# Three SwiGLU half-steps of a two-layer backbone: five groups of four tiles by quarters, and two plain tiles at the end

## The chip, the cores and the metric

The kernel runs on one core of one Trainium2 chip. The metric is the device time of one launch in microseconds (us). Engines are named as in the profile: PE is the matrix engine, PEld its weight loads, DVE the vector engine, ACT the scalar engine, POOL the third elementwise engine, SP the queue that issues most of the transfers.

## The reference, cut to what matters

Two layers run over 512 latent tokens and 256 context tokens. Each layer is a half-step SwiGLU, a token mixing, and a second half-step SwiGLU; every one of them begins with an RMSNorm that is scaled and shifted, and ends with a gated addition.

```python
def _swiglu(h, w_gu, w_down):
    a, b = jnp.split(h @ w_gu, 2, axis=-1)
    return (jax.nn.silu(a) * b) @ w_down
...
h_lat = h_lat + 0.5 * ml[2] * _swiglu(_modulate(h_lat, norm_ffn1[l], ml[0], ml[1]), ffn1_w_gu[l], ffn1_w_down[l])
h_ctx = h_ctx + 0.5 * mc[2] * _swiglu(_modulate(h_ctx, norm_ffn1[l], mc[0], mc[1]), ffn1_w_gu[l], ffn1_w_down[l])
...
mix_lat, mix_ctx = _token_mix(n_lat, n_ctx, w_in[l], w_out[l], ...)
h_lat = h_lat + ml[5] * mix_lat
h_lat = h_lat + 0.5 * ml[8] * _swiglu(_modulate(h_lat, norm_ffn2[l], ml[6], ml[7]), ffn2_w_gu[l], ffn2_w_down[l])
```

The width is 1024, the hidden width of SwiGLU 2816, which is 22 tiles of 128. The context takes no part in the second SwiGLU of layer 1, so three half-steps have 768 tokens and one has 512.

## The kernel before, in words

**Numbers.** Every float32 operand is split into a rounded high part and the remainder, and a product takes three matmuls (`mm3`: high by high, high by low, low by high). A weight tile of 128x512 arrives by a transfer into a `raw` buffer (four of them), ACT casts its high part into a `w` buffer (eight of them), and DVE or POOL subtracts to get the low part (`w_copies`, `w_subs`).

**By quarters.** A product of two operands that are cut in halves both ways needs eight block products; the kernel uses a scheme with seven and some sums before and after. The gate and up products of a pair of hidden tiles are done so (`pair`: the inner dimension and the tokens are halved, 384 tokens each; sums of the activations are made once per half-step by `t_task`, sums of the weights by POOL in `w_sums`). The first pair of a half-step is done plainly (`first_pair`), because those sums are not there yet. The down product of four hidden tiles is also done by quarters where `fast` says so: `hid_sums` forms the seven combinations of the hidden tiles (`put` splits each into high and low), `down_fast` multiplies each with its weight combination and DVE adds it to the residual `H` (`upd`). Such a group of four has 7 x 2 x 2 outputs of 128 features by 384 tokens with 2 x 3 matmuls each, which is 168 matmuls of 384 columns. The sums of its weights are POOL's.

**Plain.** Otherwise `down` multiplies the hidden tiles of the group for one output of 128 features after the other. A group in the middle does it in two chunks of 384 tokens; the last group does it in three chunks of 256 (HALF0 and HALF1 of the latent tokens, then the context, CTX), and as soon as the eight outputs of a chunk are added to `H`, the next step's norm of that chunk starts: `norm_sq` squares on ACT and sums into `nacc`, `norm_r` transposes `nacc` on PE, reduces on DVE and takes the root on POOL (`rs`), `norm_task` transposes `rs` on PE and then, for each of eight feature tiles, scales (DVE), adds the shift (DVE or ACT), casts the high part (ACT) and subtracts (DVE or POOL). PE's first products of the next step read these tiles.

**What sets the order.** The order of every engine's instructions is fixed when the kernel is written out: generators yield when the program's own estimate of time says that something is not ready, and what comes first in that estimate is written first. Each engine then runs its list in order and waits on semaphores. `segs` names the groups of a half-step: first all pairs of a segment, then its down products. Before, layer 0 uses `[(2, 4), (4,), (4,), (4,), (4,)]` and layer 1 `[(2,), (4,), (4,), (4,), (4,), (4,)]`; the rule is

```python
return n == 4 and f + n < NF and (l, which) != (1, 2)
```

so in each of the three half-steps with 768 tokens the first two tiles go down plainly, 16 by quarters, and the last four plainly in three chunks. `u` is the ring of 20 large buffers that holds activations, their sums and hidden tiles.

Of the kernel before, what the change touches and what calls it, by code (L numbers as in the profile page):

```python
# [10 lines left out]
F32R = mybir.dt.float32r  # L11
# [4 lines left out]
P = 128  # L16
# [7 lines left out]
PROJ = 2304  # L24
EPS = 1e-6
NMOD = 9
SEGA, SEGB = [(2, 4), (4,), (4,), (4,), (4,)], [(2,), (4,), (4,), (4,), (4,), (4,)]

LAT = (0, 512, 0)
CTXC = (512, 256, 1)  # L30
# [110 lines left out]
class Kernel:  # L141
# [8 lines left out]
    def __init__(self, tc, I, out, pools):  # L150
# [10 lines left out]
        self.flags = set()  # L161
        self.mcols = [16, 0]
        self.mod0 = self.rawlim = 0
        self.ulive = 0
        self.nready = {}
        self.ps = pools["ps"].tile([P, 4096], F32, tag="b", name="b", bufs=1)
# [428 lines left out]
        return n == 4 and f + n < NF and (l, which) != (1, 2)  # L595

    def segs(self, l, which):
        return SEGA if l == 0 else SEGB


    def setup(self):
# [554 lines left out]
    def hid_tiles(self, quick, f, hid):  # L1156

        if not quick or f == 0:
            x = yield from (self.uget([P, 4, self.tq]) if quick else self.uget([P, 2, TOK], F32R))
            hid.append(x)  # L1160
        return hid[-1]

# [57 lines left out]
    def pair(self, l, which, i, hid, done, quick):  # L1220
# [4 lines left out]
        def prod(no, nm, h, out, start):  # L1225
            yield (lambda: nm in self.R)
            w = yield from self.getp(("u", l, which, i, no, h))
            hi, lo = self.R[nm]
            for j in range(4):
                r = self.rdy(lo[:, j])  # L1230
                if r > self.t:
                    yield r
                c = slice(j * P, j * P + P)
                self.mm3(out[:, :tq], (w[:, 0, c], w[:, 1, c]), (hi[:, j], lo[:, j]), start and j == 0, j == 3, True)
                yield
            self.relp(w)

        def work(f, th):

# [131 lines left out]
    def ffn(self, l, which, chunks, last_chunks, next_norm):  # L1371
# [5 lines left out]
        for si, ns in enumerate(segs):  # L1377
            last = si == len(segs) - 1
            groups, i = [], f
            for n in ns:  # L1380
                hid, done, sums, quick = [], [], {}, self.fast(l, which, n, i)
                if quick:
                    self.spawn(self.hid_sums(hid, done, tq, sums), 1)
                for i in range(i, i + n, 2):
                    self.spare = i + 4 - f <= 4
                    yield from (self.pair(l, which, i, hid, done, quick) if i else self.first_pair(l, which, hid, done, quick))
                i += 2
                groups.append((n, quick, hid, done, sums))
# [6 lines left out]
            for n, quick, hid, done, sums in groups:  # L1395
# [14 lines left out]
                                if cc == order[-1] and (kt + 1) * P % w == 0:  # L1410
                                    self.relp(Ws[kt * P // w])
                else:
                    for hi, lo in self.R.values():
                        self.uf(hi, lo)
                    if which == 1:
                        self.spawn(self.mix_constants(l), 3)
                    Ws = []
# [860 lines left out]
```

## Time and profile before

| | |
|---|---|
| median of three runs | 2637.1 us (2631.66 to 2638.93) |
| the profiled execution's own time | 2629.54 us |
| its span | 2627.8 us |
| PE busy | 2539.9 us (97%) |
| DVE / POOL / ACT busy | 2033.7 (77%) / 1322.7 (50%) / 1249.9 us (48%) |
| mean granted clock of PE | 0.99 |

The page gives busy time per engine, then the span in forty slices (the granted clock in tenths of full speed), the queues of transfers, the chain of waits that ended last, and groups of instructions with their count, busy time, mean duration and the idle time before them. The three half-steps lie at 45 to 594 us, 923 to 1480 us and 1480 to 1982 us; the mixings lie between them and after the third.

### The profile page before, as it was taken

The numbers are of one execution on the slowest core, as the hardware profiler recorded it, in microseconds if no ns is written. First come the engines' busy times: TensorE is split into PE (matmuls) and PEld (weight loads), VectorE is DVE, ScalarE is ACT, GpSimd is POOL, SyncE is SP. The second block draws the span as 40 slices with busy tenths as digits, with TensorE's granted clock in tenths as the row PEclk, the third lists the DMA queues.
The fourth block names the chain that finished last, engine by engine and source line by source line (L and its number), as shares of the span: only waits on it lengthen the run. The fifth ranks groups of instructions, "written<-read, shape, count | busy, mean of one in ns | idle before, by whom it ended". The sixth has DMA issues, their size and how long they took to land.

```text
span 2627.8 us, 44905 instructions
## 1 busy us (share of the span) xinstructions
PE 2539.9 (97%) x17116; PEld 2418.3 (92%) x17116; DVE 2033.7 (77%) x3513; ACT 1249.9 (48%) x2576; POOL 1322.7 (50%) x1093
## 2 busy tenths in 40 slices
PE   7999999999999999999999989999999999999998
PEld 5888999999998978889999989999999888999998
DVE  5767787878689886776787877878878788977776
ACT  4433344456645643343444534444446655544445
POOL 3636656733232344555774547767744332644443
PEclk9999999999999999999999999999999999999999
DMA  8455322221121155553223112222222211233332
GB/s 283 141 184 180 113 73 89 65 83 57 49 65 33 57 170 176 185 170 133 76 65 97 49 49 81 65 65 75 74 87 65 61 57 40 66 96 98 99 103 72
DMA packets 193623, 252.58 MB, mean 96 GB/s; under 512 B 12188, under 2 KB 160896, under 8 KB 193408
## 3 DMA queue, kind: packets, MB, share of 16 engines
q1 hardware_dynamic: 187152, 246.82, 29.3%
q10 hardware_dynamic: 6256, 2.90, 0.4%
q8 instruction: 134, 2.20, 0.3%
q14 instruction: 81, 0.66, 0.1%
HBM read 247.59 MB, written 2.10 MB: 95 GB/s over the span
## 4 chain that ended last, share of the span: by engine, by line
PE 69%; DVE 19%; issue 3%; POOL 3%; ACT 3%; DMA 2%; SPq 0%; ACTq 0%; DVEq 0%; POOLq 0%
PE b L241 42%; PE b L243 23%; DVE u L127 8%; DVE w L127 4%; DVE t L127 4%; PE b L254 2%; DVE H L127 2%; PE b L282 2%; DMA raw<-in_ffn_w_gu_dram 1%; ACT u L127 1%; POOL w L127 1%; POOL raw L127 1%; ACT w L127 1%; ACT t L127 1%; POOL nacc L127 0%
## 5 line engine op out<-in xcount | busy, mean ns | idle before, releaser
L241 PE MATMUL b<-u,w 128*128 128x384 f32 (+1 forms) x8736 | 1447.1, 326 | 13.9 <-DVE adasum L127 6.8
L241 PEld LDWEIGHTS b<-u,w 128*128 128x128 f32 x8736 | 1425.6, 189 | 33.7 <-issue 16.7
L127 ACT CAST w<-raw 128x512 fp32r<-128x512 f32 x949 | 575.6, 620 | 572.0 <-PE b L241 199.9
L127 DVE TENSOR_TENSOR w<-raw,w 128x512 fp32r<-128x512 f32 x677 | 651.2, 972 | 233.7 <-ACT w L127 226.5
L127 POOL TENSOR_TENSOR raw<-raw 128x512 f32<-128x512 f32 x416 | 612.8, 1494 | 344.6 <-DMA raw<-in_ffn_w_gu_dram 125.7
L127 POOL TENSOR_TENSOR w<-raw,w 128x512 fp32r<-128x512 f32 x272 | 374.1, 1390 | 501.3 <-ACT w L127 454.7
L243 PE MATMUL b<-u,w 128*128 128x256 f32 (+2 forms) x3888 | 584.4, 308 | 21.8 <-ACT u L127 6.4
L243 PEld LDWEIGHTS b<-u,w 128*128 128x128 f32 x3888 | 542.6, 193 | 46.7 <-ACT u L127 7.7
L127 DVE SCALAR_TENSOR_TENSOR H<-b,modG,H 128x128 f32<-128x128 f32 (+3 forms) x832 | 364.3, 473 | 135.1 <-PE b L243 80.5
L243 PE MATMUL b<-w,u 128*128 128x256 f32 x2172 | 281.2, 286 | 1.3 <-DVE w L127 1.2
L243 PEld LDWEIGHTS b<-w,u 128*128 128x128 f32 x2172 | 271.2, 193 | 6.5 <-DVE w L127 1.7
L127 ACT CAST u<-u 128x384 fp32r<-128x384 f32 (+4 forms) x318 | 140.7, 464 | 133.0 <-DVE u L127 86.6
L127 DVE TENSOR_TENSOR u<-u 128x384 fp32r<-128x384 f32 (+8 forms) x226 | 167.9, 763 | 11.6 <-ACT u L127 10.7
L127 POOL TENSOR_TENSOR u<-u 128x384 fp32r<-128x384 f32 (+3 forms) x138 | 120.1, 880 | 95.3 <-ACT u L127 94.9
L127 ACT CAST u<-t 128x384 fp32r<-128x384 f32 (+2 forms) x162 | 74.8, 471 | 187.8 <-DVE t L127 183.1
L127 ACT COPY t<-b 128x384 f32<-128x384 f32 (+5 forms) x223 | 99.3, 446 | 122.3 <-PE b L241 78.7
L127 POOL TENSOR_TENSOR nacc<-nacc,t 128x256 f32<-128x256 f32 (+2 forms) x112 | 90.5, 808 | 102.5 <-ACT t L127 98.4
L127 DVE TENSOR_TENSOR t<-t,b 128x384 f32<-128x384 f32 (+3 forms) x216 | 105.9, 493 | 33.8 <-PE b L241 33.2
L127 DVE TENSOR_TENSOR u<-u,t 128x384 f32<-128x384 f32 (+1 forms) x105 | 102.0, 979 | 12.9 <-POOL u L127 4.8
L127 DVE TENSOR_TENSOR u<-t,u 128x384 fp32r<-128x384 f32 (+3 forms) x144 | 101.3, 709 | 10.6 <-ACT u L127 9.3
L243 PE MATMUL b<-u 128*128 128x256 f32 (+5 forms) x516 | 103.7, 334 | 3.4 <-DVE u L127 3.1
L127 DVE TENSOR_TENSOR u<-b,u 64x256 fp32r<-64x256 f32 (+3 forms) x175 | 90.9, 525 | 19.6 <-ACT u L127 17.8
(99 smaller groups left out, 1563.0 us busy)
## 6 DMA issues: line engine op xcount, KB each, us to landing
raw<-in_ffn_w_gu_dram SPq DMA_DIRECT2D x176, 512.0 KB
adaraw<-in_ada_w_dram SPq DMA_DIRECT2D x114, 512.0 KB
raw<-in_ffn_w_down_dram SPq DMA_DIRECT2D x88, 512.0 KB
raw<-in_w_in_dram SPq DMA_DIRECT2D x28, 512.0 KB
raw<-in_w_out_dram SPq DMA_DIRECT2D x32, 256.0 KB
u<-in_ada_w_dram SPq DMA_DIRECT2D x14, 512.0 KB
u<-in_ada_w_dram SPq DMA_DIRECT2D x16, 384.0 KB
raw<-in_w_in_dram SPq DMA_DIRECT2D x16, 256.0 KB
```

What stands on the lines that cost most here:

```text
L127: getattr(self.eng, name)(*args, **kw)
L241: self.nc.tensor.matmul(out, a, b, start=start, stop=stop, skip_group_check=True)
L243: self.nc.tensor.matmul(out, a, b, start=start, stop=stop)
L254: self.nc.tensor.matmul(out[q:q + 32], self.cs[:, k], x, start=start, stop=stop)
L282: self.nc.tensor.transpose(out, in_, self.ident[:p, :p])
```

## The change

The segments of the three half-steps become five groups of four, all by quarters, and the last segment has a plain group of two tiles behind its group of four: the pairs of all six tiles first, then the group's down product by quarters, then the two tiles plainly in the three chunks of 256 tokens. The first pair's hidden tiles now go down by quarters too. Two `u` buffers are taken at the start of the last segment for the plain tiles' hidden values, and the sums of the activations are given back one by one in the last pair instead of all at once behind it. The second SwiGLU of layer 1 keeps its segments.

```diff
-SEGA, SEGB = [(2, 4), (4,), (4,), (4,), (4,)], [(2,), (4,), (4,), (4,), (4,), (4,)]
+SEGF, SEGP = [(4,), (4,), (4,), (4,), (4, 2)], [(2,), (4,), (4,), (4,), (4,), (4,)]
...
     def segs(self, l, which):
-        return SEGA if l == 0 else SEGB
+        return SEGP if (l, which) == (1, 2) else SEGF
...
         if not quick or f == 0:
-            x = yield from (self.uget([P, 4, self.tq]) if quick else self.uget([P, 2, TOK], F32R))
+            if self.kept:
+                x = self.kept.pop(0)
+            else:
+                x = yield from (self.uget([P, 4, self.tq]) if quick else self.uget([P, 2, TOK], F32R))
             hid.append(x)
...
             self.relp(w)
+            if h == 1 and i == NF - 2:
+
+                self.uf(*self.R.pop(nm))
...
             groups, i = [], f
+            keep = []
+            if len(ns) > 1:
+
+                keep = yield from self.ugets(2, [P, 2, TOK], F32R)
...
                 for i in range(i, i + n, 2):
+                    self.kept = [] if quick else keep
...
                 else:
-                    for hi, lo in self.R.values():
-                        self.uf(hi, lo)
                     if which == 1:
```

**PE, end of layer 0's first half-step.** `u,w` with 256 columns are the plain down products, `nacc` and `rs` the two transposes of a chunk's norm, `w,u` the first projection of the mixing. Before:

```order
L241 MATMUL b<-u,w 128x384 x1488
L243 MATMUL b<-u,w 128x256 x111
L282 MATMUL b<-ident,nacc 128x128 x2
L243 MATMUL b<-u,w 128x256 x15
L282 MATMUL b<-ident,rs 128x128 x2
L243 MATMUL b<-u,w 128x256 x99
L282 MATMUL b<-ident,nacc 128x128 x2
L243 MATMUL b<-u,w 128x256 x18
L282 MATMUL b<-ident,rs 128x128 x2
L243 MATMUL b<-u,w 128x256 x45
L243 MATMUL b<-w,u 128x256 x42
L282 MATMUL b<-ident,nacc 128x128 x2
```

There are 288 plain matmuls. In the changed kernel there are 144 (75 and the first `nacc` stand ahead of these rows), and the context's two transposes stand between the first matmuls of the projection:

```order
L245 MATMUL b<-u,w 128x256 x18
L284 MATMUL b<-ident,rs 128x128 x2
L245 MATMUL b<-u,w 128x256 x48
L284 MATMUL b<-ident,nacc 128x128 x2
L245 MATMUL b<-u,w 128x256 x3
L245 MATMUL b<-w,u 128x256 x6
L284 MATMUL b<-ident,rs 128x128 x2
L245 MATMUL b<-w,u 128x256 x9
L284 MATMUL b<-ident,nacc 128x128 x2
L245 MATMUL b<-w,u 128x256 x9
L284 MATMUL b<-ident,rs 128x128 x2
L245 MATMUL b<-w,u 128x256 x120
```

The transposes of the first rotated projection (`ident,t`) follow directly behind the 120.

**DVE, the same place.** `u<-H,modA,b` is the scaling of a norm, `u<-u,M` its shift, `u<-u` its subtraction, `w<-raw,w` the low part of a weight tile. Before, the end of HALF1's updates:

```order
L127 SCALAR_TENSOR_TENSOR H<-b,modG,H 128x256 x2
L127 TENSOR_TENSOR w<-raw,w 128x512
L127 TENSOR_TENSOR nacc<-nacc,t 128x256
L127 SCALAR_TENSOR_TENSOR H<-b,modG,H 128x256
L127 TENSOR_TENSOR w<-raw,w 128x512
L127 TENSOR_REDUCE ms<-b 128x2
```

In the changed kernel, from the last update of the context on:

```order
L128 SCALAR_TENSOR_TENSOR H<-b,modG,H 128x256
L128 TENSOR_SCALAR modG<-M 128x16
L128 TENSOR_TENSOR w<-raw,w 128x512
L128 SCALAR_TENSOR_TENSOR u<-H,modA,b 128x256
L128 TENSOR_SCALAR u<-u,M 128x256
L128 TENSOR_TENSOR u<-u 128x256
```

At that point four of HALF0's eight scalings are still to come. From HALF0's last update to the end of the first rotation DVE's list has eight `w<-raw,w` before and four now.

**PE, from layer 0's second half-step into layer 1's first.** Before:

```order
L243 MATMUL b<-u,w 128x256 x45
L243 MATMUL b<-u,w 128x384 x42
L282 MATMUL b<-ident,nacc 128x128 x2
L243 MATMUL b<-u,w 128x384 x12
L282 MATMUL b<-ident,rs 128x128 x2
L243 MATMUL b<-u,w 128x384 x234
L241 MATMUL b<-u,w 128x384 x2352
```

Now:

```order
L245 MATMUL b<-u,w 128x256 x48
L284 MATMUL b<-ident,nacc 128x128 x2
L245 MATMUL b<-u,w 128x256 x3
L284 MATMUL b<-ident,rs 128x128 x2
L284 MATMUL b<-ident,nacc 128x128 x2
L284 MATMUL b<-ident,rs 128x128 x2
L245 MATMUL b<-u,w 128x384 x192
L243 MATMUL b<-u,w 128x384 x2520
```

The 96 plain down matmuls behind the first pair (42 + 12 + 234 are 192 of the pair and these 96) are gone, the 168 of the new group are among the 2520, and the context's transposes stand ahead of the first pair. Over the program PE has 432 matmuls of 256 columns fewer and 216 of 384 columns more; DVE has 30 `w<-raw,w` fewer, POOL 48 more of them and 24 more sums of raw tiles.

## Rows read from the trace of the kernel before

**Rows 1.** The page: busy time, share of the span, instructions of each engine.

```profile
PE 2539.9 (97%) x17116; PEld 2418.3 (92%) x17116; DVE 2033.7 (77%) x3513; ACT 1249.9 (48%) x2576; POOL 1322.7 (50%) x1093
```

**Rows 2.** The page's groups: line, engine, operation, count | busy us, mean ns | idle before.

```profile
L127 DVE TENSOR_TENSOR w<-raw,w 128x512 fp32r<-128x512 f32 x677 | 651.2, 972 | 233.7 <-ACT w L127 226.5
L127 POOL TENSOR_TENSOR raw<-raw 128x512 f32<-128x512 f32 x416 | 612.8, 1494 | 344.6 <-DMA raw<-in_ffn_w_gu_dram 125.7
L127 POOL TENSOR_TENSOR w<-raw,w 128x512 fp32r<-128x512 f32 x272 | 374.1, 1390 | 501.3 <-ACT w L127 454.7
```

**Rows 3.** PE's timeline: start us, length us, instructions merged [idle before <-releaser].

```profile
442.04 33.21 PE L241 MATMUL b<-u,w 128*128 128x384 f32 x190 [0.16 <-DVE u L127]
...
556.55 13.46 PE L243 MATMUL b<-u,w 128*128 128x256 f32 x111
569.86 0.42 PE L282 MATMUL b<-ident,nacc 128*128 128x128 f32 x2
...
595.07 3.02 PE L243 MATMUL b<-w,u 128*128 128x256 f32 x23 [0.62 <-DVE w L127]
598.45 0.44 PE L282 MATMUL b<-ident,nacc 128*128 128x128 f32 x2 [0.36 <-POOL nacc L127]
...
604.11 0.38 PE L282 MATMUL b<-ident,t 128*128 128x128 f32 x2
...
628.96 0.33 PE L282 MATMUL b<-ident,t 128*128 128x128 f32 x1 [1.81 <-DVE t L127]
```

**Rows 4.** DVE's timeline where layer 0's first half-step ends.

```profile
568.26 0.48 DVE L127 SCALAR_TENSOR_TENSOR H<-b,modG,H 128x256 f32<-128x256 f32 x1 [0.96 <-PE b L243]
...
572.33 1.26 DVE L127 SCALAR_TENSOR_TENSOR u<-H,modA,b 128x256 f32<-128x256 f32 x3 [0.45 <-PE b L282]
573.51 0.34 DVE L127 TENSOR_SCALAR u<-u,M 128x256 f32<-128x256 f32 x1
...
574.66 0.42 DVE L127 TENSOR_TENSOR u<-u 128x256 fp32r<-128x256 f32 x1
...
584.21 0.67 DVE L127 TENSOR_TENSOR w<-raw,w 128x512 fp32r<-128x512 f32 x1
...
611.38 0.42 DVE L127 TENSOR_TENSOR u<-u 128x256 fp32r<-128x256 f32 x1 [0.47 <-ACT u L127]
```

**Rows 5.** Stretches: length, busy of PE, PEld, DVE, ACT, POOL, granted clock, transfers.

```profile
168.00:221.00 53.00, 52.06 (x345) 47.33 (x346) 41.92 (x88) 15.93 (x30) 33.30 (x27) 1.00 0.48 166
386.10:474.30 88.20, 88.04 (x508) 87.72 (x507) 72.60 (x107) 38.69 (x76) 61.56 (x45) 1.00 0.24 72
568.70:611.80 43.10, 42.12 (x350) 41.61 (x349) 40.35 (x97) 26.69 (x65) 23.98 (x31) 1.00 0.17 50
1034.00:1077.00 43.00, 40.40 (x278) 35.59 (x277) 35.63 (x71) 12.27 (x23) 22.43 (x18) 1.00 0.37 124
1450.00:1481.80 31.80, 30.95 (x238) 30.40 (x237) 28.63 (x78) 20.93 (x58) 20.30 (x30) 1.00 0.01 2
1519.00:1537.00 18.00, 15.16 (x76) 14.76 (x77) 16.24 (x34) 3.00 (x5) 6.42 (x5) 0.81 0.01 2
1982.00:2022.00 40.00, 37.08 (x293) 36.20 (x291) 34.22 (x77) 25.84 (x56) 19.54 (x25) 0.96 0.23 67
```

**Rows 6.** PE's timeline, from the context's last norm to layer 1's first down product.

```profile
1482.22 0.44 PE L282 MATMUL b<-ident,nacc 128*128 128x128 f32 x2 [1.17 <-DVE nacc L127]
...
1483.13 2.20 PE L243 MATMUL b<-u,w 128*128 128x384 f32 x11 [0.29 <-POOL u L127]
...
1516.43 0.62 PE L243 MATMUL b<-u,w 128*128 128x384 f32 x2 [2.56 <-DVE u L127]
1520.12 0.69 PE L243 MATMUL b<-u,w 128*128 128x384 f32 x1 [3.07 <-ACT u L127]
1522.53 13.57 PE L243 MATMUL b<-u,w 128*128 128x384 f32 x68 [1.72 <-DVE u L127]
```

**Rows 7.** PE's timeline, first matmuls of the second pair in layer 0's two half-steps.

```profile
91.00 0.79 PE L241 MATMUL b<-u,w 128*128 128x384 f32 x3 [3.59 <-DVE adasum L127]
...
966.46 0.76 PE L241 MATMUL b<-u,w 128*128 128x384 f32 x3 [1.00 <-DVE adasum L127]
```

More of the change, by code (lines that the diff above doesn't have):

```diff
@@ L163, in __init__ @@
         self.mod0 = self.rawlim = 0
+        self.kept = []
         self.ulive = 0
```

## The prediction

> **What bounds the kernel now.** I read the page's busy times first: PE is busy 97% of the span and DVE 77% [rows 1], so time is won either by taking work from PE or by closing the places where PE waits. Then PE's timeline, to see how long a matmul takes and where the idle time stands; then the stretches, to see who is full where PE waits. In the middle of a half-step PE never stops: from 386 to 474 us, one group of four tiles with its two pairs, it is busy 88.04 of 88.20 us, while DVE is at 72.60 and POOL at 61.56 [rows 5]. At the ends it is otherwise. From the last update of HALF0 at 568.3 us to the end of the context's norm at 611.8 us [rows 4] DVE is busy 40.35 of 43.10 us and PE 42.12 [rows 5]: both are full there, and PE's own waits are small, 0.62 and 0.36 us [rows 3]. The same holds from 1450 to 1481.8 us, with 28.63 us of DVE in 31.80 [rows 5]. What I take from this: in the body of a half-step a matmul less is time won, and in the hand-over from one step to the next PE and DVE are two queues of almost equal length, so that shortening PE's alone wins only what DVE lets it win.
>
> **The change part by part.** The durations are those of the profiled execution, which took 2629.5 us and lies 7.6 us under the median of 2637.1. The sum below is a difference; I add it to the median.
>
> *Matmuls.* 190 matmuls of 384 columns take 33.21 us, 0.175 us each; 111 of 256 columns take from 556.55 to 569.86, 13.31 us, 0.120 us each [rows 3]. A half-step loses 96 of 384 columns (16.8 us) and 144 of 256 (17.3 us) and gets a group of 168 of 384 (29.4 us). That is 4.7 us less for each of three half-steps, **14.1 us less** in all, and all of it is on PE, which the chain follows.
>
> *DVE, ACT and POOL for the new group.* One more group by quarters means combinations of the hidden tiles, 28 wider updates in place of narrower ones, 24 more sums of raw weights over the program at 1494 ns and 48 more subtractions on POOL at 1390 ns [rows 2], 103 us of POOL in three half-steps, while DVE gives up 30 subtractions of 972 ns [rows 2]. I cost it at nothing: the same mix of work stands beside the group from 386 to 474 us, where DVE has 15.6 us and POOL 26.6 us to spare and PE none [rows 5]. If that cover were gone, 34 us of POOL per half-step would be the price. Transfers stay the same in bytes; buffers of `u` are given back earlier.
>
> *The first down product.* In layer 1 the two plain tiles go down behind a single pair, and PE stands still for their hidden tiles three times, 2.56, 3.07 and 1.72 us [rows 6]; the releasers are DVE and ACT, whose list is full of sums of activations at that time. Now a second pair follows, which does not need the hidden tiles: **7.4 us less**. In layer 0 the plain products behind three pairs show smaller waits: PE idles 0.94 us from 168 to 221 us and 2.60 us from 1034 to 1077 us [rows 5]. With them **3.5 us** go. In their place layer 1 gets the wait that both half-steps of layer 0 show at their second pair, 3.59 and 1.00 us [rows 7]; I take the mean, **2.3 us more**, and the two as its ends.
>
> *The hand-overs.* The plain tail shrinks from 288 to 144 matmuls, from about 35 to 17 us, but the work that DVE does in it stays: 24 updates, three norms, and the weights of what follows. The price is the difference of two queues. From HALF0's last update to the end of the norms and the first rotation DVE needs 40.35 us now [rows 5]. Four of its eight weight subtractions leave that stretch (4 x 0.97 = 3.9 us [rows 2]), and about 1.5 of its 2.75 us of idle time are the norm's chain, which stays: 38.0 us. PE has in the same stretch of the changed order 96 down matmuls and 144 of the projection, 28.8 us, and five pairs of transposes of 0.38 us [rows 3], 30.7 us in all. It waits 7.3 us where it waited 1.0 [rows 3]: **6.3 us more**. The hand-over of layer 1's first half-step is the same work, with granted clock and idle time as before (37.08 of 40 us busy) [rows 5]: **6.3 us more**. Between the layers DVE needs 28.63 us until HALF1's tiles stand [rows 5], less three subtractions (2.9 us) and plus 1.5 us, 27.2 us; PE has 96 x 0.120 + 48 x 0.175 us and four pairs of transposes, 21.4 us. It waits 5.8 us where it waited 1.17 and 0.29 [rows 6]: **4.3 us more**. Behind each, who waits is clear: PE's list has the first projection, or the first pair, right behind the transposes, and all else is queued behind those. The bounds: nothing, if DVE never holds PE longer than now (PE is busy 42.12 of 43.10 us there [rows 5]); and, if no subtraction leaves and all idle time stays, 43.1 - 30.7 - 1.0 = 11.4 us at the mixings and 31.8 - 21.4 - 1.5 = 8.9 us between the layers. I take the values above, since the rows of DVE's stretch are nearest to what is left in its list.
>
> *The granted clock.* In the two stretches with waits of PE it is 0.81 over 18 us and 0.96 over 40 us [rows 5]: part of the time the lower of the two levels, 1.2 GHz, was granted, which costs 3.4 and 1.6 us. Where PE has no waits it is 1.00. I let the new wait at the first mixing cost one such fall, **1.6 us more**, and leave the other two as they are; the ends are 3.4 us less and 6.8 us more.
>
> *The sum:* -14.1 - 7.4 - 3.5 + 2.3 + 6.3 + 6.3 + 4.3 + 1.6 = **-4.2 us**, 2632.9 us on the median: **2633 us**. A measurement of this kernel can tell about 0.3%, 7.9 us, from no change; so this is no change. With all lower ends it is -14.1 - 7.4 - 3.5 + 1.0 - 3.4 = -27.4 us, with all upper ends, the first downs' 3.5 us not won, -14.1 - 7.4 + 3.6 + 11.4 + 11.4 + 8.9 + 6.8 = +20.6 us.
>
> One row needs a word: a subtraction of DVE takes 0.67 us at 584.21 us [rows 4] and 0.97 us on average [rows 2], so something stretches it by 0.30 us. The Trainium skill, in SBUF — State Buffer, section "Who interferes with whom", says that a DVE instruction with two inputs in SBUF and a POOL instruction that reads SBUF exclude each other for their whole length, which speaks against moving work to POOL. By that rule each of the four subtractions that leave DVE at a hand-over would come back as one stretched instruction there; the trace has the stretch but not its cause.
>
> **The rivals.**
>
> *DVE yields (0.28).* If the norm's subtractions and the later weights move out of the way, PE waits half of what I took: 8.5 us less, and the low clock between the layers goes, 3.4 us: -16.1 us, 2621 us. For it speaks that POOL is busy only 23.98 of 43.10 us in the hand-over [rows 5]. Against it: the order still gives DVE four or five of the eight subtractions of each norm.
>
> *DVE's list decides (0.22).* The context's norm is the mechanism: its two transposes now stand between, or ahead of, the first matmuls of what follows, and its sum stands in DVE's list behind HALF0's scalings, so PE starts the next step only when DVE is through. At the upper prices of the hand-overs (31.7 in place of 16.9 us) and of the clock (6.8 in place of 1.6 us), 3.6 us at the second pair: -14.1 - 7.4 - 3.5 + 3.6 + 31.7 + 6.8 = +17.1 us, 2654 us. It decides from about 29 us of waits in the three hand-overs on, which is 12 us more than I took.
>
> *The wait at layer 1's first pair only moves (0.12).* The second pair needs the sums of the activations early, and DVE is full when it makes them. If PE waits there as long as it did for the hidden tiles, 7.4 us come back: +3.2 us, 2640 us. Layer 0's second pair, with 3.59 us at most [rows 7], speaks against it.
>
> *POOL stretches DVE (0.06).* Four subtractions per hand-over at 0.30 us are 1.2 us, 3.6 us for three: -0.6 us, 2637 us. This is the rule named above.
>
> That the change does nothing is excluded by the order, which has the 432 and 216 matmuls.
>
> **How the numbers follow.** The forecast has 0.32. Its own range is about 8 us to either side, so 0.06 of it lies beyond 0.3% on the fast side and 0.02 on the slow side. Faster is 0.28 + 0.06 = 0.34, slower 0.22 + 0.02 = 0.24, and the rest, 0.42, within 0.3%. The range takes in the fast rival's 2621 and stops just short of the slow rival's full price, of which the half is likelier than the whole: 2619 to 2651 us.
>
> **What would show it.** In the changed profile: groups of 168 matmuls in 29 us with PE full in all five groups; PE's first matmuls of both mixings waiting some 7 us in all on DVE or on tiles of `u`, and those of layer 1's first pair 6 us; DVE full for 38 us behind HALF0; no waits of 2 to 3 us behind layer 1's first pair; a granted clock under 1.00 at three places. PE busy about 14 us less. It would be wrong if the hand-overs cost under 8 or over 29 us in all, or if a new group's down product waits for its combinations.

## The result, and the profile after

The changed kernel takes 2649.6 us (median of six runs, 2647.8 to 2655.4) beside 2634.8 us of the kernel before (six runs, 2631.5 to 2638.9): a ratio of 1.0059, interval 1.0045 to 1.0074. It is 15 us slower, where 4 us less and "no change" were forecast; the time lies inside the range, on the other side of zero.

The page after, busy times and the three groups that answer to [rows 1, 2]:

```profile
PE 2544.3 (96%) x16900; PEld 2417.4 (91%) x16900; DVE 2071.0 (78%) x3579; ACT 1270.0 (48%) x2611; POOL 1438.8 (54%) x1166
...
L128 POOL TENSOR_TENSOR raw<-raw 128x512 f32<-128x512 f32 x440 | 650.1, 1497 | 328.2 <-DMA raw<-in_ffn_w_gu_dram 133.1
L128 DVE TENSOR_TENSOR w<-raw,w 128x512 fp32r<-128x512 f32 x647 | 636.5, 996 | 215.6 <-ACT w L128 205.9
L128 POOL TENSOR_TENSOR w<-raw,w 128x512 fp32r<-128x512 f32 x320 | 446.2, 1409 | 455.3 <-ACT w L128 422.7
```

The instructions moved as forecast: 216 matmuls fewer, 24 sums and 48 subtractions more on POOL, 30 subtractions fewer on DVE. But PE, which should have been busy 14 us less, is busy 4.4 us more. The spans, 2648.5 and 2627.8 us, show why: PE is idle 104.2 us in place of 87.9, 16.3 us more, and its mean granted clock is 0.983 in place of 0.990. Work 14.1 us less and busy time 4.4 us more means 18.5 us lost to the lower clock; the means say the same (0.017 x 2648.5 - 0.010 x 2627.8 = 18.7). **-14.1 + 16.3 + 18.5 = 20.7 us**, the whole difference of the two spans. The split is that of these two executions, which lie some 6 us further apart than the medians: the profiled one has the lowest clock of its six (0.983 to 0.986, mean 0.985), while 99 executions of the kernel before, measured beside the experiments, have 0.986 to 0.992, mean 0.989. By these means the clock costs about 11 us, and by subtraction the waits about 18, of the 15 us between the medians.

Where, DVE's timeline tells: the last update of `H` in each half-step and the first of each mixing. After:

```profile
590.31 0.47 DVE L128 SCALAR_TENSOR_TENSOR H<-b,modG,H 128x256 f32<-128x256 f32 x1
...
812.56 0.75 DVE L128 SCALAR_TENSOR_TENSOR H<-b,modG,H 128x512 f32<-128x512 f32 x1
...
1481.76 0.48 DVE L128 SCALAR_TENSOR_TENSOR H<-b,modG,H 128x256 f32<-128x256 f32 x1
...
1994.61 0.47 DVE L128 SCALAR_TENSOR_TENSOR H<-b,modG,H 128x256 f32<-128x256 f32 x1
```

The stretches between such rows, in us, from one profiled execution each (the last two columns are experiments below; a half-step that an edit does not reach differs by up to 3.8 us between executions, as in layer 0's first one between the changed kernel and the run without layer 1's weight sums; the first mixing's stretch agrees to 0.1 us where the instructions are the same):

| stretch | before | after | new front, old tail | old front, short tail |
|---|---|---|---|---|
| start to end of layer 0's first half-step | 593.7 | -3.4 | +1.7 | -0.8 |
| from there to the first mixing's first update | 214.8 | +7.5 | 0.0 | +8.4 |
| from there to the end of layer 0's second half-step | 668.0 | +1.2 | +6.8 | -3.3 |
| from there to the end of layer 1's first half-step | 505.6 | +7.2 | +2.3 | +12.6 |
| from there to the second mixing's first update | 182.9 | +6.5 | +1.2 | +6.9 |
| from there to the last update | 451.9 | +2.3 | +1.5 | +2.0 |

PE's timeline after, where new waits stand. First the mixing, then between the layers, then the new first group's down product in layer 0's second half-step and in layer 1:

```profile
591.24 0.43 PE L284 MATMUL b<-ident,rs 128*128 128x128 f32 x2 [1.45 <-POOL rs L128]
592.59 0.58 PE L245 MATMUL b<-w,u 128*128 128x256 f32 x1 [0.69 <-DVE u L128]
593.92 1.60 PE L245 MATMUL b<-w,u 128*128 128x256 f32 x5 [0.75 <-ACT u L128]
...
1483.75 0.43 PE L284 MATMUL b<-ident,rs 128*128 128x128 f32 x2 [2.38 <-POOL rs L128]
1488.83 0.69 PE L284 MATMUL b<-ident,nacc 128*128 128x128 f32 x2 [4.66 <-DVE nacc L128]
1491.67 0.69 PE L284 MATMUL b<-ident,rs 128*128 128x128 f32 x2 [2.15 <-POOL rs L128]
...
1012.10 6.02 PE L243 MATMUL b<-u,w 128*128 128x384 f32 x24 [3.53 <-DVE adasum L128]
1022.82 4.44 PE L243 MATMUL b<-u,w 128*128 128x384 f32 x16 [3.70 <-DVE adasum L128]
...
1567.38 1.32 PE L243 MATMUL b<-u,w 128*128 128x384 f32 x6 [3.02 <-ACT u L128]
1570.90 3.57 PE L243 MATMUL b<-u,w 128*128 128x384 f32 x10 [2.21 <-DVE u L128]
```

In layer 1 those waits are for combinations of hidden tiles (`u`). In layer 0 the profile puts the release at `adasum`, the modulation's sum, which reads a PSUM bank that PE writes, and stands in DVE's list behind two of the combinations; DVE's timeline ahead of the matmuls at 1022.82:

```profile
1019.29 3.15 DVE L128 TENSOR_TENSOR u<-u,t 128x384 f32<-128x384 f32 x2
1022.36 0.41 DVE L128 TENSOR_TENSOR adasum<-adasum,b 128x256 f32<-128x256 f32 x1
```

And the stretches around the four places, then one ahead of each of the two down products (columns as in [rows 5]):

```profile
590.00:602.60 12.60, 9.34 (x37) 7.93 (x38) 11.91 (x31) 8.00 (x21) 8.73 (x11) 0.59 0.17 44
1484.00:1497.00 13.00, 6.19 (x21) 5.20 (x20) 11.50 (x37) 8.66 (x26) 9.31 (x15) 0.61 0.27 81
1011.00:1026.00 15.00, 10.20 (x50) 9.30 (x51) 9.83 (x18) 3.75 (x9) 5.37 (x5) 0.77 0.39 138
1567.00:1576.00 9.00, 6.42 (x23) 6.10 (x24) 8.90 (x19) 4.65 (x10) 6.94 (x6) 0.62 0.22 60
...
985.00:1011.00 26.00, 23.57 (x165) 20.75 (x163) 19.24 (x23) 10.23 (x21) 18.31 (x12) 1.00 0.50 168
1528.00:1542.00 14.00, 14.00 (x83) 14.00 (x82) 13.76 (x11) 4.25 (x10) 11.40 (x7) 1.00 0.00 0
```

At these four places, where PE waits several times in a few microseconds, the granted clock is 0.59 to 0.77, that is, 1.2 GHz for a half to four fifths of the stretch. At the first mixing PE waits only 3.5 us in these and a small fourth wait, while the clock's share of the 12.60 us is 5.2 us (0.41 of them). Not every cluster of waits brings the lower level: in layer 0's first half-step waits of 1.88, 0.85 and 1.01 us between 131 and 144 us left the clock at 1.00 (from 128 to 155 us).

### The profile page after: what moved, and what is told of

The parts are those of the page before. It is cut to its first block, busy times and chain, and to the rows that moved or that the text cites. A ratio compares the mean times of both kernels' runs of the same rounds, so it can differ in the third digit from the quotient of the medians.

```text
span 2648.5 us, 44775 instructions
## 1 busy us (share of the span) xinstructions
PE 2544.3 (96%) x16900; PEld 2417.4 (91%) x16900; DVE 2071.0 (78%) x3579; ACT 1270.0 (48%) x2611; POOL 1438.8 (54%) x1166
## 4 chain that ended last, share of the span: by engine, by line
PE 67%; DVE 20%; POOL 4%; ACT 4%; issue 4%; DMA 2%; ACTq 0%; SPq 0%; DVEq 0%; POOLq 0%
PE b L243 46%; PE b L245 18%; DVE u L128 9%; DVE w L128 5%; DVE t L128 4%; PE b L256 2%; POOL nacc L128 2%; ACT u L128 2%; PE b L284 1%; ACT w L128 1%; DVE H L128 1%; ACT t L128 1%; POOL raw L128 1%; POOL w L128 1%; POOL u L128 1%
## 5 line engine op out<-in xcount | busy, mean ns | idle before, releaser
L243 PE MATMUL b<-u,w 128*128 128x384 f32 (+1 forms) x9240 | 1545.1, 327 | 28.1 <-DVE adasum L128 12.3
L243 PEld LDWEIGHTS b<-u,w 128*128 128x128 f32 x9240 | 1519.5, 189 | 52.6 <-issue 18.5
L128 POOL TENSOR_TENSOR raw<-raw 128x512 f32<-128x512 f32 x440 | 650.1, 1497 | 328.2 <-DMA raw<-in_ffn_w_gu_dram 133.1
L128 POOL TENSOR_TENSOR w<-raw,w 128x512 fp32r<-128x512 f32 x320 | 446.2, 1409 | 455.3 <-ACT w L128 422.7
L128 DVE SCALAR_TENSOR_TENSOR H<-b,modG,H 128x128 f32<-128x128 f32 (+3 forms) x892 | 388.4, 473 | 138.4 <-PE b L243 81.6
L245 PE MATMUL b<-u,w 128*128 128x256 f32 (+2 forms) x3168 | 479.3, 309 | 16.5 <-ACT t L128 5.3
L128 ACT CAST u<-u 128x384 fp32r<-128x384 f32 (+4 forms) x354 | 157.7, 468 | 157.6 <-DVE u L128 103.2
L128 DVE TENSOR_TENSOR u<-u 128x384 fp32r<-128x384 f32 (+7 forms) x268 | 199.1, 764 | 16.8 <-ACT u L128 15.6
L128 POOL TENSOR_TENSOR u<-u 128x384 fp32r<-128x384 f32 (+4 forms) x138 | 123.2, 901 | 105.0 <-ACT u L128 98.5
L128 ACT CAST u<-t 128x256 fp32r<-128x256 f32 (+2 forms) x144 | 65.7, 466 | 157.8 <-DVE t L128 152.8
L128 POOL TENSOR_TENSOR rs<-mse,mhalf 128x2 f32<-128x2 f32 (+4 forms) x41 | 43.5, 1063 | 116.9 <-DVE mse L128 111.3
```

The source lines that it names most:

```text
L128: getattr(self.eng, name)(*args, **kw)
L243: self.nc.tensor.matmul(out, a, b, start=start, stop=stop, skip_group_check=True)
L245: self.nc.tensor.matmul(out, a, b, start=start, stop=stop)
```

## The experiments

Times are ratios to the kernel before, measured beside it; 0.1% is 2.6 us.

**Front and tail apart.** The segments of the three half-steps, nothing else. Front alone:

```diff
-SEGF = [(4,), (4,), (4,), (4,), (4, 2)]
+SEGF = [(4,), (4,), (4,), (4,), (2,), (4,)]
```

> Five groups of four by quarters from the start, as in the change, but the last segment is two plain tiles first and the last group of four plainly in three chunks, as before: matmuls as many as before, hand-overs as before. Theory A (the first group's down product, which now stands behind two pairs only, waits because DVE is still behind with the sums of activations): PE waits 3 to 4 us there in layer 0's first half-step, 7 to 11 us in its second and about 5 us in layer 1's, against 0.9, 2.6 and 7.4 us that go; with the clock 6 to 10 us slower than the kernel before, 2641 to 2645 us. Rival B (the short tail alone costs, the new front does what was forecast): the waits of 7.4 and 3.5 us go and nothing comes but 2.3 us, 8 us faster than before, about 2627 us.

Tail alone:

```diff
+SEGF = [(2, 4), (4,), (4,), (4,), (2,), (2,)]
+SEGG = [(2,), (4,), (4,), (4,), (4,), (2,), (2,)]
-        return SEGP if (l, which) == (1, 2) else SEGF
+        return SEGP if (l, which) == (1, 2) else SEGF if l == 0 else SEGG
```

> The groups at the start of each half-step as in the kernel before (three pairs, or one pair, and then two plain tiles), and only two tiles in the last plain segment, two more plain tiles ahead of it. Matmuls as before to 0.5 us per half-step. Theory A: the three hand-overs cost as in the changed kernel, 7.5, about 5 and 6.6 us, and the first down products wait as before: 16 to 20 us slower than the kernel before, about 2652 us. Rival B (the short tail is the whole cost): the same or more, 20 us and up, since all of the loss must come back here. Rival C (the front is the whole cost): within 5 us of the kernel before.

Measured: 1.0043 (1.0031 to 1.0054) and 1.0109 (1.0092 to 1.0126). Both cost: the front 11 us, the tail 29 us, and neither saves matmuls, since each has four groups by quarters per half-step, as before (the first expectation says five, which is a slip). Less the 14.1 us of matmuls they make 26 us by the medians and 25 by the stretches, where the change has 15 and 21: in layer 1, where both make PE wait in the same stretch, +2.3 and +12.6 stand, with 4.7 us of matmuls saved, against +7.2. Rival B falls by the front's 11 us and Rival C by the tail's 29; but Theory A had 16 to 20 us for the tail, and 29 is more than it explains. PE's timeline of the front alone, in layer 0's second half-step and in layer 1, shows the waits at the first group and, in layer 1, at the first pair by quarters:

```profile
1007.68 6.00 PE L243 MATMUL b<-u,w 128*128 128x384 f32 x24 [2.97 <-DVE adasum L128]
...
1018.40 3.83 PE L243 MATMUL b<-u,w 128*128 128x384 f32 x12 [3.72 <-DVE adasum L128]
...
1533.96 29.79 PE L243 MATMUL b<-u,w 128*128 128x384 f32 x162 [5.98 <-DVE u L128]
1565.61 2.72 PE L243 MATMUL b<-u,w 128*128 128x384 f32 x14 [1.85 <-DVE u L128]
```

and that of the tail alone, between the layers, where the sum had 4.3 us and PE waits 9.4 us where it waited 1.5:

```profile
1480.59 0.44 PE L285 MATMUL b<-ident,nacc 128*128 128x128 f32 x2 [1.32 <-DVE nacc L129]
1483.92 0.43 PE L285 MATMUL b<-ident,rs 128*128 128x128 f32 x2 [2.90 <-POOL rs L129]
1487.71 0.69 PE L285 MATMUL b<-ident,nacc 128*128 128x128 f32 x2 [3.36 <-DVE nacc L129]
1490.22 0.69 PE L285 MATMUL b<-ident,rs 128*128 128x128 f32 x2 [1.82 <-POOL rs L129]
```

**Does a second pair hide the wait?** The kernel before, with layer 0's segments in layer 1 too.

```diff
-        return SEGA if l == 0 else SEGB
+        return SEGB if (l, which) == (1, 2) else SEGA
```

> The kernel before with one change: in layer 1's first half-step the two plain tiles go down behind three pairs, as they do in layer 0, in place of behind the first pair. Theory A (a first down product waits as long as it stands too near to the norm): the waits of 2.56, 3.07 and 1.72 us and the half clock behind them go, 3.4 us more, and a wait at the second pair of 1.0 to 3.6 us comes: 7 to 10 us faster than the kernel before, 2625 to 2628 us. Rival D (DVE is full there whatever PE's order, so the wait only moves to the second pair's sums of activations): within 3 us of the kernel before.

1.0014 (1.0006 to 1.0023), 4 us slower: Rival D, a little over its 3 us. The waits for hidden tiles go and others come at the second pair. PE's and DVE's timelines of this kernel:

```profile
1512.39 3.82 PE L241 MATMUL b<-u,w 128*128 128x384 f32 x12 [2.55 <-DVE t L127]
1523.91 3.57 PE L241 MATMUL b<-u,w 128*128 128x384 f32 x10 [7.71 <-DVE t L127]
```

```profile
1514.13 7.59 DVE L127 TENSOR_TENSOR u<-u 128x768 fp32r<-128x768 f32 x4
1521.65 1.74 DVE L127 TENSOR_TENSOR w<-raw,w 128x512 fp32r<-128x512 f32 x1
1523.32 0.54 DVE L127 TENSOR_TENSOR t<-t,b 128x384 f32<-128x384 f32 x1
```

The product of SiLU at 1523.32 reads the last bank of the first pair; the matmul that needs the bank starts right behind it. Ahead of it stand four low parts of sums (T2 and T4) that PE needs later.

**That order alone.** In the next three, T2 and T4 are split only when the first pair's four products of SiLU are written out: with three pairs in layer 1, in the changed kernel, in the kernel before.

```diff
         self.any2("tensor_mul", sv, sv, uv)
+        self.nmul += 1
...
             hi, lo = yield from self.ugets(2, [P, 4, tq], F32R)
+            yield (lambda: self.nmul >= 4)
```

> The experiment with three pairs at the start of layer 1, and there, as in the other half-steps, the low parts of the second pair's last two sums (four DVE instructions of 768 columns, 7.59 us in a row at 1514 us) stand behind the products of SiLU that give PE's banks back, in place of ahead of them. Theory Q (the wait of 7.71 us is a queue on DVE: the bank that PE needs hangs behind four instructions that are not yet needed): that wait and the half clock behind it go, 8 to 12 us faster than without it, about 2627 us and 4 to 8 us faster than the kernel before. Rival A (DVE has too much to do there, and any order makes PE wait): what goes at the bank comes back at the third product, within 3 us of the 2636.8 us.

> The changed kernel with the same order of DVE at the second pair. Theory Q: the changed kernel's waits at the first group's down product (5.2 us in layer 1, 7.2 us in layer 0's second half-step) do not hang on these four instructions, those at the second pair are small already: within 4 us of the changed kernel. Rival: DVE's queue of four instructions sets the whole delay of the front: 8 us faster and more, 2641 us.

> The kernel before with the same order of DVE at the second pair of each half-step. Theory Q: in layer 1 PE waits for hidden tiles of the first pair (2.56, 3.07 and 1.72 us), whose products of SiLU and low parts now come before the four instructions: 3 to 7 us of these waits and of the half clock go, 2627 to 2630 us. Rival A: they come back at the third product of the second pair; within 3 us of the kernel before.

0.9982 (0.9971 to 0.9993), 1.0042 (1.0028 to 1.0055) and 0.9991 (0.9981 to 1.0001). With three pairs 8 us come back and the waits shrink to 3.62 and 1.19 us: Theory Q. The kernel before wins 2 us, which is not told from none, and not the 3 to 7 us of Theory Q. So with this order three pairs in layer 1 are worth about 2 us against one pair (0.9982 beside 0.9991), which is not told from none either. The changed kernel wins 4.5 us, at the edge of what can be told; but its trace shows where. In layer 0's second half-step, where the expectation had the waits stay, they go from 3.53 and 3.70 us to these, and the stretch is 5.1 us shorter:

```profile
1004.90 2.38 PE L243 MATMUL b<-u,w 128*128 128x384 f32 x12 [1.60 <-ACT u L128]
1008.02 4.69 PE L243 MATMUL b<-u,w 128*128 128x384 f32 x24 [0.75 <-DVE adasum L128]
1016.12 7.58 PE L243 MATMUL b<-u,w 128*128 128x384 f32 x42 [1.16 <-DVE adasum L128]
```

In layer 1 its waits at the first group's down product are 1.36 and 2.22 us, where the changed kernel has 3.02 and 2.21. So the order of DVE's list is a good part of the front's price in layer 0 and a small one in layer 1.

**POOL beside DVE.** The changed kernel without the sums of raw weights of layer 1's first half-step.

```diff
-                    self.G(op, out, a, b)
+                    if key[1:3] != (1, 1):
+                        self.G(op, out, a, b)
```

> The changed kernel without POOL's sums of raw weights for layer 1's first half-step (the products there are made with weights that are not summed; PE, DVE and ACT have the same instructions). Theory P (DVE is late at the front because POOL's sums stretch its instructions: between 1482 and 1580 us the instructions that lie beside POOL take 15 to 19 us longer there than their like without POOL): the waits of 9.2 us between the layers shrink to 5 to 8 us, those of 5.2 us at the first group's down product go, and with the clock that half-step and the mixing behind it are 8 to 14 us shorter, about 2638 us. Theory A alone (DVE's list is too long, stretched or not): under 4 us are won, 2646 to 2650 us. The same instructions of DVE should be at 0.55 and 0.68 us there in place of 1.0 to 1.7.

1.0027 (1.0012 to 1.0043), 8 us faster than the changed kernel. PE's timeline from between the layers to past the first group's down product, and then the same 48 us of the second pair and that product in the changed kernel (first row) and here:

```profile
1492.51 0.69 PE L284 MATMUL b<-ident,nacc 128*128 128x128 f32 x2 [4.66 <-DVE nacc L128]
1495.35 0.69 PE L284 MATMUL b<-ident,rs 128*128 128x128 f32 x2 [2.15 <-POOL rs L128]
1495.81 14.71 PE L245 MATMUL b<-u,w 128*128 128x384 f32 x74
1511.34 20.81 PE L245 MATMUL b<-u,w 128*128 128x384 f32 x118 [0.82 <-DVE w L128]
1531.98 68.28 PE L243 MATMUL b<-u,w 128*128 128x384 f32 x393
```

```profile
1532.00:1580.00 48.00, 42.52 (x231) 41.55 (x230) 42.85 (x62) 20.86 (x42) 32.60 (x24) 0.93 0.17 55
```

```profile
1535.70:1583.70 48.00, 48.00 (x279) 48.00 (x278) 36.97 (x70) 22.04 (x43) 25.72 (x19) 1.00 0.29 88
```

The front's waits are gone, as Theory P had it. Those between the layers stand to the hundredth, but that decides nothing: the first sum left out stands at 1514 us in POOL's list, and up to there the two kernels have the same instructions. DVE does more instructions in less time; its weight subtractions, in the groups of DVE in these 48 us, changed kernel and this one:

```profile
L128 DVE TENSOR_TENSOR w<-raw,w 128x512 fp32r<-128x512 f32 x12 | 11.8, 1006 | 4.0 <-ACT w L128 3.9
```

```profile
L128 DVE TENSOR_TENSOR w<-raw,w 128x512 fp32r<-128x512 f32 x8 | 5.5, 690 | 6.5 <-ACT w L128 6.5
```

Layer 0's half-steps, whose sums stayed, keep their waits at 1014 and 1025 us (3.7 us each). The sums themselves are also off the path of the weights here, so this run does not part the stretching from their lateness; the durations show that there is stretching, not how much of the 8 us is its.

**The hand-overs.** Five edits of the changed kernel. First the context's norm held until HALF1's tiles are done:

```diff
+        if cc == CTXC and self.R is not None and HALF1 in self.xfull:
+            yield (lambda: self.xfull[HALF1] == KT)
```

> The changed kernel, in which the context's norm that feeds a half-step by quarters is held until all eight tiles of HALF1 are done; it bears on the second half-step of layer 0 and the first of layer 1. Rival E (the place of the context's transposes, ahead of the first pair's matmuls, makes the waits of 2.38, 4.66 and 2.15 us between the layers and the half clock of 10 us behind them): the waits shrink to under 3 us and the clock stays whole there, 8 to 11 us faster than the changed kernel, about 2640 us. Theory A (DVE has too long a list, and the place of the transposes only chooses where PE waits): what goes there comes back at the first pair of quarters or the first group's down product, within 4 us of the changed kernel, 2646 to 2653 us.

1.0074 (1.0062 to 1.0086): Rival E falls. PE waits for HALF1's tiles in place of the context's transposes, and again at the first pair by quarters:

```profile
1488.74 7.17 PE L245 MATMUL b<-u,w 128*128 128x384 f32 x24 [6.84 <-ACT u L128]
...
1538.56 30.02 PE L243 MATMUL b<-u,w 128*128 128x384 f32 x162 [6.82 <-DVE u L128]
```

Then the additions of squares in `norm_sq` (`self.G`, POOL): moved to DVE for the context, or for HALF1; six of seven left out for the context, or for both.

```diff
-                (self.G if self.mod0 == KT else self.any2)("tensor_add", acc[:, :n], acc[:, :n], prev)
+                (self.V if cc == CTXC and self.mod0 == KT else self.G if self.mod0 == KT else self.any2)("tensor_add", acc[:, :n], acc[:, :n], prev)
```

(with `HALF1` in place of `CTXC` for the other), and left out, with `in (HALF1, CTXC)` for both:

```diff
-            if prev is not None:
+            if prev is not None and not (self.mod0 == KT and cc == CTXC):
```

> The changed kernel, in which the sums of squares of the context's norm (seven additions of 128x256, one after the other) are DVE's at every hand-over, and not POOL's. Theory N (with the short tail the context's updates come faster than POOL adds their squares, 0.74 to 0.9 us each, and the root of HALF1 stands in POOL's list behind them: the waits of 2.38 and 4.66 us between the layers and of 1.45 us at the mixings are POOL's chain): they shrink to about 1.2, 2.5 and 0.8 us, 4 to 9 us faster than the changed kernel, 2641 to 2646 us. Theory D (DVE's list is what PE waits for, as the prediction reckoned it): DVE gets 2.9 us more at each of the hand-overs and nothing is won, 0 to 6 us slower than the changed kernel.

> The changed kernel, in which the context's sum of squares at each hand-over leaves out six of its seven additions (the squares are still made; six additions of 0.74 to 0.9 us, 4.5 to 5.5 us of POOL per hand-over, are gone, and the root of HALF1 no longer stands behind them). Theory S (between the layers PE waits for a chain of single steps, and its longest link is the context's additions): the wait of 4.66 us falls under 1 us and that of 2.38 us to about 1.5; 5 to 9 us faster than the changed kernel, 2640 to 2645 us. Theory D (HALF1's tiles, which DVE, ACT and POOL make, are as late in any case, and the wait goes on to them, as the run with the context held showed with 6.84 us): under 3 us faster.

> The same with six of HALF1's seven additions left out as well. If the hand-over is a chain that begins with HALF1's sum of squares, then HALF1's root comes 4 us sooner here and the waits between the layers go down to under 3 us, those at the mixings to under 2 us, 10 us and more faster than the changed kernel, 2639 us or less. If it is DVE's list of scalings, shifts and low parts (38 us of work beside 31 us of PE at a mixing, as the prediction reckoned it), the time goes down by less than 4 us, and PE waits for tiles of u instead.

> The changed kernel with HALF1's seven additions of squares made by DVE at every hand-over, where POOL made them (0.41 in place of 0.75 us each), the context's left on POOL. If the hand-over hangs on how soon HALF1's root is there, and POOL's pace is the cause, half or more of the 8.6 us that leaving them out gave comes here too: 4 to 8 us faster than the changed kernel, 2640 to 2645 us, and the stretch from the last update to the first output of the mixing is 3 to 5 us shorter. If DVE's list is as long a chain as POOL's, the 2.9 us that it gets at each hand-over eat this up: within 3 us of the changed kernel.

| additions of squares | ratio to before | first mixing | second mixing |
|---|---|---|---|
| changed kernel | 1.0059 | +7.5 | +6.5 |
| context's on DVE | 1.0054 (1.0041 to 1.0068) | +6.2 | +6.7 |
| context's left out | 1.0050 (1.0033 to 1.0067) | +5.8 | +5.2 |
| HALF1's and context's left out | 1.0027 (1.0015 to 1.0039) | +2.5 | +2.0 |
| HALF1's on DVE | 1.0088 (1.0075 to 1.0101) | +9.3 | +8.2 |

The hand-over at a mixing hangs in good part on HALF1's norm: without the context's additions 1.7 of 7.5 us come back, without HALF1's as well 5.0. With both left out the kernel is 8 us faster than the changed one, between the 10 us of the chain and the 4 us of DVE's list. The waits are then 0.2 to 0.5 us each and the clock does not fall (the stretch around the same place without both):

```profile
584.00:612.00 28.00, 25.77 (x199) 24.06 (x199) 27.55 (x75) 21.35 (x53) 12.81 (x17) 1.00 0.07 20
```

But quicker additions are no cure when DVE has to make them: DVE adds in 0.41 us what takes POOL 0.75, and with HALF1's additions there the kernel is 8 us slower than the changed one, where the expectations had 4 to 8 us faster or no change. PE waits 3.23 us in one piece for a tile of DVE. DVE is busy 11.91 of 12.60 us at this place in the changed kernel, so a link that is moved onto it delays the next:

```profile
593.88 0.58 PE L245 MATMUL b<-w,u 128*128 128x256 f32 x1 [3.23 <-DVE u L128]
```

Theory N (4 to 9 us faster) and Theory S (5 to 9 us) fall: with the context's additions on DVE or left out the kernel is 1 and 2 us faster than the changed one, within the noise. Between the layers the wait of 4.66 us goes to 3.91 us without the context's additions, not under 1 us; without HALF1's as well PE waits 1.46 and 3.83 us, the longer one for tiles of `u`. What sets these last is open.

**What was found, together.** The changed kernel with the later sums, the context's squares on DVE, and the sums of layer 1's first raw weights on DVE; then three versions on the long tail and three pairs: the context's squares on DVE; those first raw weights on DVE; the context's squares on DVE and HALF1's on whichever engine the program's estimate has free (`self.any2`). The sums of raw weights, in `w_sums`, as edited on the long tail (on the short tail the choice also takes in the first down group):

```diff
+            E = self.V if key[1:3] == (1, 1) and key[0] == "u" and key[3] in (2, 4) else self.G
...
-                    yield (lambda: self.G.t <= self.t + 300.0)
-                    self.G(op, out, a, b)
+                    yield (lambda: E.t <= self.t + 300.0)
+                    E(op, out, a, b)
```

> The changed kernel with all that the experiments found: the second pair's sums later, the context's sums of squares on DVE, and the raw weights of layer 1's first two pairs by quarters and first down group summed on DVE. Theories N and P together: 8 to 14 us faster than the changed kernel, 2635 to 2642 us, no slower than the kernel before by more than 0.2%. Rival (what is left is the length of the lists of DVE): at best the 2645 us that the first of these alone gave.

> The fastest version so far (long tail as before, three pairs in layer 1, the second pair's last two sums later) with the context's sums of squares on DVE. Theory N: with the long tail the chain has time enough, and PE waits only 1.19 us for it between the layers: within 2 us of it, 2628 to 2631 us. Theory D: 3 to 6 us slower, since DVE is full at the hand-overs.

> The fastest version so far, in which the sixteen sums of raw weights of the first two pairs by quarters of layer 1's first half-step are DVE's in place of POOL's. Theory P (beside POOL an instruction of DVE with two inputs in SBUF takes up to 1 us longer, so a sum on POOL costs DVE more than the 0.68 us that it takes on DVE itself): the waits of 3.62, 1.19 and 0.81 us at the second and third pair shrink, 2 to 5 us faster. Rival (DVE is full there, and what it gets it has to do): 3 to 8 us slower.

> The fastest version so far (long tail, three pairs in layer 1, the second pair's sums later, the context's squares on DVE) with HALF1's additions on DVE or POOL, whichever the program's estimate has free first. With the long tail PE waits little for HALF1's root (no wait over 1.2 us between the layers): within 3 us of it, 2627 to 2633 us.

1.0027 (1.0016 to 1.0038) for the first: the findings give back 8 us of 15. The others are 0.9980 (0.9970 to 0.9990), 0.9984 (0.9975 to 0.9993) and **0.9969 (0.9958 to 0.9980)**; the last, 2624.4 us beside 2632.9 and a little under what was expected, beats both kernels, by 0.3% and, through the two ratios, 0.9%. It has the groups of the kernel before in layer 0 and layer 0's groups in layer 1's first half-step; the rest of it is order, and who adds the squares. The middle two are not told from the 0.9982 that they start from, so neither the context's squares nor the place of the first weight sums decides with a long tail; the last is the best of the four, but its interval overlaps theirs too.

## Why the prediction was wrong

**The step that failed is "The first down product"**, with its companion, the new group's work on DVE, ACT and POOL "at nothing". They had 7.4 and 3.5 us go and 2.3 us come, -8.6 us. The front alone measures +1.7 + 6.8 + 2.3 = **+10.8 us**: 19 us of error. In the change itself, with 4.7 us of matmuls per half-step and 12.8 us for the hand-over between the layers (7.7 us of waits and 5.1 of clock) taken out, the same three stretches leave about 6 us: still 15 us of error. It is not the amount of work, since the front alone has as many groups as the kernel before and front and tail together cost no less than the change. Two things were taken from the wrong place. The cover was read as spare time in the middle of a half-step, 15.6 us of DVE from 386 to 474 us [rows 5]; but the new group's down product stands at the front, and there it did not cover. In layer 1 DVE had none to spare ahead of it (13.76 us of 14.00 from 1528 to 1542 us), and without POOL's sums beside it the waits went. In layer 0 DVE had no less of its time in hand than in the middle (it was busy 19.24 us of 26.00 from 985 to 1011 us), and PE waited all the same, for an instruction late in DVE's list; the other order took back half of these waits. And the old waits [rows 6] were read as waits for hidden tiles that another pair would hide; with three pairs (the third experiment) they came back as waits for banks. That was a rival, "the wait at layer 1's first pair only moves", at 0.12. With the order mended too, the pairs were worth 2 us of the 7.4, not told from none.

**The granted clock** was taken at 1.6 us and cost 18.5 us in the profiled execution, about 11 by the means of all: that term was mis-sized. The sum priced waits and treated the clock as a remark on one of them. Not all of it is lost time: in the run with the context held, whose instructions are the same up to 1488 us, the clock there is 0.73 over the same 12.60 us, not 0.59, and the stretch is as long (+7.5 us), since PE then waits 0.66 us for a weight tile of DVE at 611 us.

**The hand-overs** were right in size at the mixings, 6.3 + 1.6 and 6.3 us against 7.5 and 6.5, though the shares differ: PE waits about 3.5 us in place of 7.3 at the first, and most of the rest is the lower clock; that the two make up the forecast is partly luck. DVE is through with the norms and the first rotation in 36.8 us (578.4 to 615.2 us), near the 38.0, but busy for only 33.57 of them. Between the layers the term was 4.3 us, with 8.9 us as its bound, and the tail alone shows 12.6 us over the stretch that begins there: the two queues were compared by their lengths, but the releasers of the waits are single steps of a chain (HALF1's root, the context's sum, the context's root). That the chain, and not the lists, sets the whole price is not shown: leaving out additions of it gave back only a part.

**The matmuls** were right: 216 fewer, and the stretches of front and tail alone add up to those of the change with -14.1 us, to 4 us; that is within what the stretches vary, and the medians, 26 against 15 us, agree less well.

By its own test ("under 8 or over 29 us" for the hand-overs, or a new group's down product that waits for its combinations) the forecast was refuted by the second part, in layer 1: the hand-overs, about 28 us with their clock where the tail alone was shortened, stand at the upper end. The slow rival, "DVE's list decides", named the hand-overs rightly; its +17 us lies near the result, but in it the front still won, so it is right in size by two errors, which is luck.

The stretching of DVE by POOL, the smallest rival, was weighed at 0.30 us for an instruction and is larger. In the changed kernel the weight subtraction takes 0.69 us in the 281 cases in which no POOL instruction runs beside it and 1.23 us on average in the other 366, while an update of 128x256, which reads PSUM, takes 0.48 us in both (sorted by overlap in the trace). The rule of the Trainium skill (SBUF — State Buffer, "Who interferes with whom") agrees with that: it has a DVE instruction with two SBUF inputs contend with a POOL instruction that reads SBUF, and one with at most one SBUF input not. Weighed there by four instructions at each hand-over, it was applied to the wrong place: the run without POOL's sums shows it at the front. What it costs by itself, apart from the sums coming late, is open.

## What to carry to other kernels

Take the spare time of an engine from the stretch in which the new work will stand, not from the body of the loop: here DVE had 15.6 us in hand in the middle of a half-step and almost none ahead of the new group in layer 1. And look at the order of its list as well: in layer 0 it had time in hand, and PE waited for one late instruction. Where PE is nearly full, give the lower clock a term of its own beside the waits: here 16.3 us of new idle time came with 11 to 18.5 us of it. Shortening the work that covers a norm does not shorten the chain of the norm; moving a link of it to a full engine made it longer.

## What was not expected of the hardware

With waits of 0.6 to 1.5 us, four within 5 us, the granted clock was 0.59 over 12.6 us at the first mixing, and 0.73 with nearly the same waits in two other runs with the same instructions up to there (the context held, and no weight sums in layer 1); in the run without HALF1's squares, waits of 0.2 to 0.5 us at the same place left it at 1.00 over 28 us. The same instruction with two SBUF inputs ranged from 0.67 to 1.79 us in one kernel; with no POOL instruction beside it, it stayed under 0.70 us.
